# One more drain of GpSimd ahead of the last two reciprocal roots of a decoder layer

## The chip, the core and the metric

The kernel runs on one core of a Trainium2 chip. The metric is the device time of one execution in microseconds (us). Engines are named as in the profile: PE is TensorE (matrix products), DVE is VectorE, ACT is ScalarE, POOL is GpSimd, SP is SyncE, which here only issues transfers. A letter q behind an engine's name means its sequencer: the instructions that handle semaphores, drains and transfers and not data. Each engine works through its own queue in the order in which the program lists its instructions, and waits for the others through semaphores. A *drain* is an instruction that holds an engine's queue until the work issued before it on that engine is done.

## The reference

One layer of a decoder on 256 tokens of width 2048, in float32:

```
h = rmsnorm(x);  p = h @ w_in
A = dilated sliding-window attention (8 heads, three configurations merged)
B = latent attention (8 heads, low-rank q and kv, shared rotary key)
x = x + rmsnorm(concat(A, B) @ w_out)
u = square(relu(rmsnorm(x) @ w_up))          # 256 x 8192
x = x + rmsnorm(u @ w_down)                  # 256 x 2048, the output
```

rmsnorm(y) is y times 1/sqrt(mean(y*y) + 1e-6), row by row, times a gain. The change lies in the last line: the product with w_down and the norm behind it.

## The kernel before

Every float32 product is made of three products of halves: a value is split into hi (ACT rounds it, line 293) and lo (DVE takes the rest, line 294), and PE adds hi*hi, hi*lo and lo*hi (line 283). The weights come from memory as tiles called raw, on SP's queue. Some blocks of the two large products are done with seven products in place of eight ("seven" in the code); the sums that this needs take weights in pairs, which come through **GpSimd's queue** into tiles ab, ab_down, c and uT (line 360).

The product with w_down is made in two halves of 1024 output columns (c = 0, 1 in the code). In the first half the split of u is made by ACT and DVE and the lo part is kept in memory (ukeep); in the second half ACT makes hi again and GpSimd fetches lo back (line 935, tile ulo). In the same way line 390 fetches kept sums back (tile s). These three lines, 360, 935 and 390, hold all transfers that GpSimd issues. The last of them is the lo part of the last group of 512 rows (g = 15).

The last two groups of the second half (g = 14 and 15) come at the end, in the loop that the change touches. Its order is written out by hand: for each block b of 128 tokens and each half n of the columns it lists PE's products for four row blocks. In group 14 the seven-product part is then added by DVE (line 1214), and behind the first of these stands the fetch of group 15's lo part. In group 15 (products on line 1141) each finished quarter is squared and summed by ACT (line 1083) and multiplied with the gain by DVE (line 1087). When both quarters of a token block are done, `final(b)` makes the norm: DVE adds the sums up (lines 1092, 1093 and 1097, the last into t_fin), **GpSimd takes the reciprocal root** (line 1098, tile rstd_fin, one for each token block, hence two in all), DVE multiplies and adds the old x in five pieces (line 1104), and SP stores each piece (line 1106).

Behind `final`, the program closes: on the profile this is line 1248, where the layer's context ends. Each engine has a drain there and reports to a common semaphore; SP first waits for the landing of the last transfers; GpSimd waits for all engines, releases them, clears the semaphores, and the engines meet once more. No line of the kernel's own code is written for this.

On GpSimd's queue, from the last fetch on, there are: the fetch of ulo for group 15, the root for token block 0, the root for token block 1, and the closing.

Of the kernel before, what the change touches and what calls it, by code (L numbers as in the profile page):

```python
# [103 lines left out]
GT = FF // 512  # L104
# [146 lines left out]
def layer(nc, tc, io):  # L251
# [49 lines left out]
    def tok(t, k, b):  # L301
        return t[:, k, b * P:(b + 1) * P]
# [623 lines left out]
    def split_u(c, g):  # L926
        if (c, g) == (0, 0):
            uh, ul = [wp.tile([P, CW], F32R, tag=w, bufs=W_BUFS, name=f"u{w}0").rearrange("p (k s) -> p k s", k=4)
                      for w in ("hi", "lo")]
        else:  # L930
            uh, ul = [dpl["dp"].tile([P, 4, S], F32R, tag=f"u{w}", bufs=2, name=f"u{w}{c}_{g}") for w in ("hi", "lo")]
        u, h, l = [x.rearrange("p k s -> p (k s)") for x in (uT[g], uh, ul)]
        if c and g:
            nc.scalar.activation(h, u, AF.Copy)
            nc.gpsimd.dma_start(out=l.bitcast(F32), in_=ukeep[g])
        else:
            split(h, l, u)
        return uh, ul
# [134 lines left out]
    def down_mm(c, u, k, b, n, w, first, last):  # L1073
        three(y[b][2 * c + n], [tok(u[x], k % 4, b) for x in range(2)], [t[:, 0, n * 512:n * 512 + 512] for t in w],
              first, last)
# [5 lines left out]
    def square(n, b):  # L1081
        junk = dpl["dp"].tile([P, 512], BF16, tag="junk", bufs=1, name=f"junkd{n}{b}")
        nc.scalar.activation(junk, y[b][n], AF.Square, accum_out=ssd[b][:, n:n + 1])

    def gain(n, b):
        yg[n, b] = spare(2 * b, n)
        nc.vector.tensor_tensor(out=yg[n, b], in0=y[b][n], in1=spare(4, n), op=OP.mult)

    def final(b):

        part = con.tile([P, 2], F32, name=f"part{b}")
        nc.vector.reduce_sum(part[:, 0:1], ssd[b][:, 0:3], axis=mybir.AxisListType.X)
        nc.vector.tensor_scalar(part[:, 1:2], part[:, 0:1], 1.0 / D, EPS, op0=OP.mult, op1=OP.add)
        square(3, b)
        t = con.tile([P, 1], F32, tag="rs_f", bufs=2, name=f"t_fin{b}")
        r = con.tile([P, 1], F32, name=f"rstd_fin{b}")
        nc.vector.tensor_scalar(t, ssd[b][:, 3:4], 1.0 / D, part[:, 1:2], op0=OP.mult, op1=OP.add)
        nc.gpsimd.tensor_tensor(out=r, in0=t, in1=neg_half, op=OP.pow)
        gain(3, b)
        yield 0  # L1100
        for n, o, w in OUT_PIECES:
            c = slice(n * 512 + o, n * 512 + o + w)
            x = spare(6 + 2 * b, n)[:, o:o + w]
            nc.vector.scalar_tensor_tensor(out=x, in0=yg[n, b][:, o:o + w], scalar=r, in1=x,
                                           op0=OP.mult, op1=OP.add)
            nc.sync.dma_start(out=io["out"][b * P:(b + 1) * P, c], in_=x)
            yield 0
# [30 lines left out]
    def three_more(out, a, w):  # L1138

        for x, z in ((0, 0), (0, 1), (1, 0)):  # L1140
            nc.tensor.matmul(out, a[x], w[z], start=False, stop=(x, z) == (1, 0), skip_group_check=True)
            flow.spend(MM)
# [7 lines left out]
    for c in range(2):  # L1150
# [5 lines left out]
        for t, (what, k, tiles) in enumerate(wide_d[c]):  # L1156
            g = (2 * k if what == "w" else k) // 4
# [40 lines left out]

    tail = {k: tiles[0] for what, k, tiles in wide_d[1] if k >= 4 * (GT - 2) and what == "k"}
    for g in (GT - 2, GT - 1):  # L1200
        for b, n in PARTS:
            for kk in range(4):
                k = 4 * g + kk
                w = weights.get(tail[k])
                if g < GT - 1:
                    down_mm(1, us[1, g], k, b, n, w, False, kk == 3)
                else:
                    three_more(y[b][2 + n], [tok(us[1, g][x], kk, b) for x in range(2)],
                               [t[:, 0, n * 512:n * 512 + 512] for t in w])
                if (b, n) == PARTS[-1]:  # L1210
                    weights.free(tail[k])
                flow.pump()
            if g < GT - 1:
                nc.vector.tensor_tensor(out=y[b][2 + n], in0=y[b][2 + n], in1=more[b, n], op=OP.add)
                if (b, n) == (0, 0):
                    us[1, g + 1] = split_u(1, g + 1)
            elif n == 0:
                square(2, b)
                gain(2, b)
            else:  # L1220
                fin = flow.start(final(b))
# [22 lines left out]
def build(nc, arrays):  # L1244
    io = {n: nc.dram_tensor(f"in_{n}", a.shape, mybir.dt.from_np(a.dtype), kind="ExternalInput").ap()
          for n, a in arrays.items()}
    io["out"] = nc.dram_tensor("out_0", (S, D), F32, kind="ExternalOutput").ap()
    with tile.TileContext(nc) as tc, tc.manual_schedule():
        layer(nc, tc, io)
# [12 lines left out]
```

## Time and profile before

| what | value |
| --- | --- |
| device time, median of 3 runs | 1055.2 us (1055.2 to 1055.52) |
| span of the profiled execution, first to last instruction | 1053.8 us |
| mean granted clock of PE in it | 0.997 |
| busy: PE, DVE, ACT, POOL | 1040.8, 811.1, 625.1, 61.5 us |
| transfers issued by GpSimd | 98 |
| last fetch issued by GpSimd | at 1020.47 us |
| the two roots begin | at 1038.97 and 1044.40 us |
| last instruction of DVE ends | at 1047.8 us |

For the profiled execution the profile gives the span and no device time of its own; the runs' median is 1.4 us longer than that span. Times within the profile count from the span's start. A row of a timeline gives start, length, engine, line, operation, the tile written and the tiles read, and in brackets how long the engine had been idle and what ended that. Matrix products overlap, so PE's busy time is not PE at its peak. The page doesn't count semaphore, drain and transfer-issuing instructions as busy; they are found by asking for their line.

### The profile page before, as it was taken

To read this page: it belongs to the slowest core of one execution; us is meant where nothing else is said; L and a number is where in the kernel's file an instruction comes from. 1 tells how busy PE (TensorE), PEld (TensorE's weight loads), DVE (VectorE), ACT (ScalarE), POOL (GpSimd) and SP (SyncE) were. 2 spreads that over 40 slices of the span, in tenths; PEclk is the share of its full clock that TensorE was granted. 3 is DMA by queue.
4 is the path that set the end of the run, shared out by engine and by line. 5 is a ranking of instruction groups with operands and counts; after the bars stand their busy time and mean duration, and the time that the engine had idled before them with its cause. 6 is when DMAs were issued, how large, how long until landed. Compare 5 with 4: busy or idle time off the path is not lost.

```text
span 1053.8 us, 13458 instructions
## 1 busy us (share of the span) xinstructions
PE 1040.8 (99%) x4854; PEld 867.4 (82%) x4854; DVE 811.1 (77%) x1080; ACT 625.1 (59%) x834; POOL 61.5 (6%) x116
## 2 busy tenths in 40 slices
PE   9999999999999999999999999999999999999996
PEld 6888889888888788888888888888888888888884
DVE  6676536567557679879888798887899987989994
ACT  6584536565555467566665666566666664666671
POOL 0000000000000000000000100000000001212100
PEclk9999999999999999999999999999999999999998
DMA  9974447454447295647556466469779767789952
GB/s 296 361 233 146 143 130 241 143 162 159 140 171 231 78 347 167 224 142 239 185 198 200 154 222 217 139 223 318 256 274 317 263 216 271 254 297 327 375 167 80
DMA packets 80644, 229.34 MB, mean 218 GB/s; under 512 B 7617, under 2 KB 12225, under 8 KB 80193
## 3 DMA queue, kind: packets, MB, share of 16 engines
q1 hardware_dynamic: 65888, 176.45, 49.3%
q0 software_dynamic: 14112, 51.39, 14.2%
q8 instruction: 38, 0.62, 0.2%
q10 hardware_dynamic: 576, 0.64, 0.2%
q14 instruction: 30, 0.24, 0.1%
HBM read 212.72 MB, written 15.73 MB: 217 GB/s over the span
## 4 chain that ended last, share of the span: by engine, by line
PE 96%; DVE 1%; issue 1%; DMA 0%; ACT 0%; POOL 0%; DVEq 0%; POOLq 0%; ACTq 0%
PE y L283 26%; PE acc_u L283 25%; PE acc_o L283 8%; PE m L283 5%; PE md L283 5%; PE acc_qk L283 4%; PE acc_v L283 4%; PE acc_ckv L283 2%; PE acc_ukv L283 2%; PE acc_q L283 2%; PE acc_cq L283 2%; PE acc_k L283 2%; PE acc_uq L283 2%; PE rt L287 1%; PE sc_b L283 1%
## 5 line engine op out<-in xcount | busy, mean ns | idle before, releaser
L294 DVE TENSOR_TENSOR lo<-raw,hi 128x1024 fp32r<-128x1024 f32 (+3 forms) x213 | 241.8, 1152 | 92.5 <-ACT hi L293 91.9
L293 ACT ACTIVATE hi<-raw 128x1024 fp32r<-128x1024 f32 (+3 forms) x213 | 209.4, 999 | 78.3 <-PE y L283 20.8
L283 PE MATMUL acc_u<-hi,hT_hi 128*128 128x512 f32 x386 | 153.4, 397 | 0.0
L283 PE MATMUL acc_u<-hi,hT_lo 128*128 128x512 f32 x386 | 150.9, 391 | 0.4 <-DVE hT_lo L294 0.4
L283 PE MATMUL acc_u<-lo,hT_hi 128*128 128x512 f32 x386 | 150.5, 390 | 0.0
L283 PE MATMUL y<-hi,uhi 128*128 128x512 f32 x376 | 146.6, 390 | 0.0
L283 PE MATMUL y<-hi,ulo 128*128 128x512 f32 x376 | 146.3, 389 | 0.0
L283 PE MATMUL y<-lo,uhi 128*128 128x512 f32 x376 | 146.3, 389 | 0.0
L298 DVE SCALAR_TENSOR_TENSOR lo<-raw,gcol,hi 128x1024 fp32r<-128x1024 f32 x86 | 107.6, 1281 | 10.6 <-ACT hi L297 10.3
L297 ACT ACTIVATE hi<-raw,gcol 128x1024 fp32r<-128x1024 f32 x86 | 97.6, 1151 | 26.6 <-PE acc_u L283 13.2
L283 PEld LDWEIGHTS acc_u<-hi,hT_lo 128*128 128x128 f32 x386 | 72.5, 188 | 16.1 <-DVE hT_lo L294 0.8
L283 PEld LDWEIGHTS acc_u<-hi,hT_hi 128*128 128x128 f32 x386 | 72.6, 188 | 14.3 <-DVE c L1008 0.4
L283 PEld LDWEIGHTS acc_u<-lo,hT_hi 128*128 128x128 f32 x386 | 72.6, 188 | 14.2
L283 PEld LDWEIGHTS y<-hi,ulo 128*128 128x128 f32 x376 | 70.6, 188 | 14.6
L283 PEld LDWEIGHTS y<-hi,uhi 128*128 128x128 f32 x376 | 70.6, 188 | 14.6
L283 PEld LDWEIGHTS y<-lo,uhi 128*128 128x128 f32 x376 | 70.6, 188 | 14.5
L283 PE MATMUL acc_o<-hi,mixT_hi 128*128 128x512 f32 x128 | 51.8, 405 | 0.0
L294 DVE TENSOR_TENSOR lo<-st_down,hi 128x1024 fp32r<-128x1024 f32 x40 | 48.1, 1221 | 4.0 <-ACT hi L293 3.8
L283 PE MATMUL acc_o<-hi,mixT_lo 128*128 128x512 f32 x128 | 50.2, 392 | 0.0
L283 PE MATMUL acc_o<-lo,mixT_hi 128*128 128x512 f32 x128 | 50.0, 391 | 0.0
L293 ACT ACTIVATE hi<-st_down 128x1024 fp32r<-128x1024 f32 x40 | 42.1, 1052 | 11.1 <-PE y L283 9.5
L293 ACT ACTIVATE hi<-ab 128x512 fp32r<-128x512 f32 (+1 forms) x38 | 31.9, 842 | 28.2 <-PE acc_u L283 21.7
(322 smaller groups left out, 1989.3 us busy)
## 6 DMA issues: line engine op xcount, KB each, us to landing
raw<-in_w_down SPq DMA_DIRECT2D x88, 512.0 KB, 6.2
raw<-in_w_up SPq DMA_DIRECT2D x86, 512.0 KB, 4.5
raw<-in_w_in SPq DMA_DIRECT2D x55, 512.0 KB, 5.0
ab<-in_w_up POOLq DMA_DIRECT2D x36, 512.0 KB, 4.8
raw<-in_w_out SPq DMA_DIRECT2D x32, 512.0 KB, 4.4
ab_down<-in_w_down POOLq DMA_DIRECT2D x20, 512.0 KB, 6.7
ukeep<-ulo SPq DMA_DIRECT2D x15, 512.0 KB, 7.2
ulo<-ukeep POOLq DMA_DIRECT2D x15, 512.0 KB, 5.3
```

The lines of the kernel that those rows point to most:

```text
L283: nc.tensor.matmul(out, a, b, start=start, stop=stop)
L287: nc.tensor.transpose(out, a, ident)
L293: nc.scalar.activation(hi, src, AF.Copy)
L294: nc.vector.tensor_tensor(out=lo, in0=src, in1=hi.bitcast(F32), op=OP.subtract)
L297: nc.scalar.activation(hi, src, AF.Copy, scale=g)
L298: nc.vector.scalar_tensor_tensor(out=lo, in0=src, scalar=g, in1=hi.bitcast(F32), op0=OP.mult, op1=OP.subtract)
```

## The change

One instruction is added, `nc.gpsimd.drain()`. It is issued once, when the loop reaches the last group, g = GT - 1 = 15. At that point all of GpSimd's transfers have been listed and the two roots haven't. Nothing else differs.

```diff
     tail = {k: tiles[0] for what, k, tiles in wide_d[1] if k >= 4 * (GT - 2) and what == "k"}
     for g in (GT - 2, GT - 1):
+        if g == GT - 1:
+            nc.gpsimd.drain()
         for b, n in PARTS:
             for kk in range(4):
                 k = 4 * g + kk
```

## The prediction

> **What bounds the kernel now.** I began with the profile's page. The lines are the span, PE's busy time, the make-up of the chain that ended last, and (from the chain in order of time) its last pieces: start, length, what.
>
> ```profile
> span 1053.8 us, 13458 instructions
> ...
> PE 96%; DVE 1%; issue 1%; DMA 0%; ACT 0%; POOL 0%; DVEq 0%; POOLq 0%; ACTq 0%
> ```
> ```profile
> 1044.37 0.59 POOLq L1248
> ...
> 1046.39 1.45 DVE uT L1104 x3
> ```
>
> PE carries 96% of the chain, so up to the last product the kernel is bound by TensorE. But this chain stops at 1046.39 + 1.45 = 1047.84 us, and the span at 1053.8. The last 6 us hold no arithmetic, and a change on GpSimd has to be read there. Line 1248 is where the program closes (queues are emptied, the engines meet, semaphores are cleared). So next I asked for that line's instructions by short stretches; columns are engine, operation, count, then shortest, median and longest duration in ns, then first and last start. The first fence is the stretch 1044.9 to 1046, the second 1048 to 1051, the third 1051.05 to 1051.06, the fourth 1053.08 to 1053.09, the fifth 1053.1 to 1053.4.
>
> ```profile
> L1248 POOLq DRAIN  x1: 8672/8672/8672, 1044.4 to 1044.4; - x1
> L1248 DVEq DRAIN  x1: 2901/2901/2901, 1045.0 to 1045.0; - x1
> ```
> ```profile
> L1248 SPq EVENT_SEMAPHORE  x9: 28/28/28, 1048.5 to 1050.9; - x9
> ```
> ```profile
> L1248 SPq DRAIN  x1: 7/7/7, 1051.1 to 1051.1; - x1
> ```
> ```profile
> L1248 POOLq EVENT_SEMAPHORE  x1: 17/17/17, 1053.1 to 1053.1; - x1
> ```
> ```profile
> L1248 POOLq DRAIN  x1: 102/102/102, 1053.3 to 1053.3; - x1
> ```
>
> DVE's closing drain ends at 1045.0 + 2.9 = 1047.9, with DVE's last instruction. SP waits for the landing of the output, then reports with a 7 ns drain that lies at 1051.05 to 1051.06 (it appears in that stretch, not in the one before). GpSimd's closing drain begins at 1044.37 (the chain's row gives the hundredths), right behind its last reciprocal root, and ends at 1044.37 + 8.67 = **1053.04**. GpSimd's event semaphore, where the engines meet, comes at 1053.08. So GpSimd is the last to arrive, 2.0 us after SP. The waits of SP's queue say the same from the other side; its longest wait there is 2.2 us (the view names PE's queue as releaser, which had long been done):
>
> ```profile
> SPq L1248 <- PEq L1248: 2.7, 2, 2.2
> SPq L1248 <- DMA out<-uT: 1.9, 1, 1.9
> ```
>
> **What is in those 8.67 us?** The timeline of GpSimd: start, length, line, work, and in brackets the idle time before it.
>
> ```profile
> 1010.27 0.72 POOL L935 DMA_DIRECT2D ulo<-ukeep  x1 [9.66 <-PE y L283]
> 1020.47 0.54 POOL L935 DMA_DIRECT2D ulo<-ukeep  x1 [9.48 <-PE y L283]
> 1038.97 0.56 POOL L1098 TENSOR_TENSOR rstd_fin<-t_fin,neg_half 128x1 f32<-128x1 f32 x1 [17.96 <-DVE t_fin L1097]
> 1044.40 0.54 POOL L1098 TENSOR_TENSOR rstd_fin<-t_fin,neg_half 128x1 f32<-128x1 f32 x1 [4.87 <-DVE t_fin L1097]
> ```
>
> The second root ends at 1044.94, so 8.1 us of the drain follow it with no arithmetic on the engine. GpSimd has issued six groups of transfers by then, and its only other drains are the program's opening one (186 ns, before any transfer) and those behind the long one (102 ns above):
>
> ```profile
> L360 POOL DMA_DIRECT2D ab<-in_w_up x36 | 19.6, 544 | 250.6 <-DVE lo L294 222.9 <-DVE c L963 27.7
> L360 POOL DMA_DIRECT2D ab_down<-in_w_down x20 | 10.7, 538 | 111.5 <-PE acc_u L283 58.7 <-DVE lo L294 52.8
> L935 POOL DMA_DIRECT2D ulo<-ukeep x15 | 8.2, 550 | 111.0 <-PE y L283 91.9 <-DMA raw<-in_w_down 10.3 <-PE md L283 8.8
> L360 POOL DMA_DIRECT2D uT<-in_w_down x12 | 6.4, 538 | 0.0
> L360 POOL DMA_DIRECT2D c<-in_w_down x8 | 4.3, 538 | 64.1 <-DVE lo L294 55.8 <-DVE acc_u L909 8.3
> L390 POOL DMA_DIRECT2D s<-skeep x7 | 3.8, 538 | 52.8 <-PE md L283 52.8
> ```
> ```profile
> L1257 POOLq DRAIN  x1: 186/186/186, 0.3 to 0.3; - x1
> ```
>
> 36 + 20 + 15 + 12 + 8 + 7 = 98 transfers. The last was issued at 1020.47, and its landing time (below) is 6.2 us, so all had landed by 1026.7, 18 us before the drain. The drain therefore isn't waiting for data. My reading: it goes through the transfers issued since the last drain, 8.1 us / 98 = 83 ns each (an estimate from these rows); drains with none to go through take 0.1 to 0.2 us. That the drain behind the long one takes 102 ns says that what has been gone through once isn't gone through again.
>
> **The change, part by part.** One instruction is added, nothing is removed or moved. It stands on GpSimd's queue between the issue at 1020.47 and the root at 1038.97.
>
> *The early drain itself.* Its price isn't in the trace at this place. Lower bound: 0.2 us (no transfers). Upper bound: it first waits out the last transfer and only then goes through all 98. The landing, from the DMA view of 1019 to 1027 (KB, us to landing):
>
> ```profile
> ulo<-ukeep POOLq DMA_DIRECT2D x1, 512.0 KB, 6.2
> ```
>
> That is 1020.47 + 6.2 + 8.67 = 1035.3. I take the going-through as overlapped with the flight: 1020.5 + 8.7 = 1029.2. Either way GpSimd would have sat idle until 1038.97 (18 us, the root's row), so the cover is 3.6 to 9.8 us wide and the drain costs 0. Queued behind it are the two roots only; for them wait DVE's L1104 and then SP's stores. If the cover were gone, DVE has 0.83 us more before its next step is late:
>
> ```profile
> 1044.11 0.21 DVE L1097 TENSOR_SCALAR t_fin<-ssd,part 128x1 f32<-128x1 f32 x1 [0.83 <-ACT junkd L1083]
> ```
>
> So the drain would have to last beyond 1039.8, over 19 us, to delay the end.
>
> *The closing drain.* Ends of its price: 8.67 us (nothing taken over) and 0.6 us (the root's 0.54 us and 0.1 for an empty drain). I take the low end, as the 102 ns row is nearest: after the early drain only the root stands before it. It then ends near 1045.0, and GpSimd no longer arrives last. Little of this is needed: SP is last from the point where the closing drain ends before 1051.06, that is where 2.0 of its 8.1 us go (24 of 98 transfers at 83 ns).
>
> *What is late next.* SP, with the landing of the output: 1051.06. One hand-over to GpSimd follows; the nearest row is t_fin's end (1044.32) to the root's start (1044.40), 0.08 us, and 0.04 us lie between the long drain's end and the event semaphore. I take 0.05, with ends 0.02 and 0.1. The meeting comes at 1051.11 in place of 1053.08, and the 0.7 us behind it (1053.08 to 1053.8) follow unchanged. **Sum: -1.97 us**, span 1051.8.
>
> Does SP's arrival itself move? The long drain runs through the second half of the output's stores and not the first. DMA views, 1040 to 1043 (first half) and 1045 to 1048.45 (second):
>
> ```profile
> out<-uT SPq DMA_DIRECT2D x3, 256.0 KB, 2.6
> out<-uT SPq DMA_DIRECT2D x2, 128.0 KB, 2.7
> ```
> ```profile
> out<-uT SPq DMA_DIRECT2D x3, 256.0 KB, 2.5
> out<-uT SPq DMA_DIRECT2D x2, 128.0 KB, 2.7
> ```
>
> The same within 0.1, so the drain slows no stores, and taking it away speeds none. Single landings differ by 0.3 either way, which is the spread I give the sum.
>
> The span of the profiled execution is 1053.8 us; the runs' median, 1055.2, lies 1.4 above it, for what is outside the span. I leave that 1.4 alone: 1055.2 - 1.97 = **1053.2 us** (-0.19%).
>
> **The rivals.**
>
> *A. The 8.1 us have nothing to do with transfers that came before.* A drain of GpSimd behind arithmetic could have this price by itself, or could wait for the output's stores (the last SP wait is at 1050.9) plus 2 us. For: only one long drain exists, so a count of transfers as its cause isn't shown. Against: the drains of 0.1 and 0.19 us stand on the same engine, the first behind memsets. Then the early drain is hidden, the closing one still ends at 1053.04: 1055.2 us.
> The Trainium skill bears on this case: "PSUM — Partial Sum Buffer", Engine vs sequencer instructions, says that a "drain waits for the engine to go fully idle". By that alone the closing drain would end at 1044.94 and the early one at 1021.0; the long drain's row ends 8.1 us later, so either the trace doesn't agree or the engine wasn't idle in a way that the profile shows. Taken as it stands the rule gives no reason why an early drain should shorten the late one, which is this rival's 1055.2.
>
> *B. The early drain keeps DVE out (slower).* If going through the transfers blocks DVE's access to its operands, the block falls where the last weights are being split:
>
> ```profile
> 1017.79 3.49 DVE L294 TENSOR_TENSOR lo<-raw,hi 128x1024 fp32r<-128x1024 f32 x3
> 1021.65 1.23 DVE L294 TENSOR_TENSOR lo<-raw,hi 128x1024 fp32r<-128x1024 f32 x1 [0.37 <-ACT hi L293]
> 1022.79 2.28 DVE L1008 TENSOR_TENSOR uT<-md,uT 128x512 f32<-128x512 f32 x3
> 1025.10 0.69 DVE L1008 TENSOR_TENSOR uT<-uT,md 128x512 f32<-128x512 f32 x1
> 1025.70 2.35 DVE L294 TENSOR_TENSOR lo<-raw,hi 128x1024 fp32r<-128x1024 f32 x2
> 1027.97 1.29 DVE L1214 TENSOR_TENSOR y<-y,uT 128x512 f32<-128x512 f32 x2
> ```
> ```profile
> 1032.25 0.39 PE L1141 MATMUL y<-hi,uhi 128*128 128x512 f32 x1
> ```
>
> A block of 8.67 us from 1021.28 lasts to 1029.95; then 1.23 + 2.28 + 0.69 + 2.35 + 0.65 = 7.2 us remain to the first L1214, which ends at 1037.15 and not 1028.6. PE needs it at 1032.25 and stands 4.9 us; less the 1.97 at the end, +2.9: 1058.1 us. It decides from a block of 3.6 + 2.0 = 5.6 us on. Against it: DVE's L1104 runs before (1039 to 1043) and during (1044.9 to 1048) the long drain:
>
> ```profile
> L1104 DVE SCALAR_TENSOR_TENSOR uT<-c,rstd_fin,uT 128x512 f32<-128x512 f32 x2 | 1.4, 748 | 0.1
> ```
> ```profile
> L1104 DVE SCALAR_TENSOR_TENSOR uT<-c,rstd_fin,uT 128x512 f32<-128x512 f32 x2 | 1.4, 750 | 0.1
> ```
>
> 748 and 750 ns: no block. The Trainium skill ("SBUF — State Buffer", SBUF: two separate sides) has such a rule: GpSimd and a DVE instruction with two SBUF inputs take a shared port pair as "an exclusive lock, not a bandwidth split". L1104 has two such inputs, and the trace shows no lock by this drain.
>
> *C. The early drain lasts over 19 us* (its price grows beside the running transfers). At thrice 8.1 us it ends at 1044.8, both roots and the stores come 5 us later, SP arrives at 1056.1 and is last: 3.0 us slower, 1058.2. Nothing in the trace speaks for it.
>
> **How the numbers follow.** Forecast 0.76, A 0.17, B 0.05, C 0.02. The forecast's own range is 1052.6 to 1053.8 (the 0.3 of the landings, doubled, for one profiled execution against many timed ones). The range reaches up to A, since A alone holds 0.17: 1052.6 to 1055.4. A measurement of this kernel tells 0.2%, 2.1 us, from no change. The forecast's 1.97 lies just inside that: I give it 0.43 of being measured beyond (0.43 x 0.76 = 0.33). Faster 0.33; same 0.61 (the rest of the forecast, 0.43, with A, 0.17, and 0.01 of rounding); slower 0.06.
>
> **What the profile after would show.** Right: the three GpSimd drains on line 1248 and the new one, which is long (8 to 15 us) and begins near 1020.5; the first root still near 1039; the closing drain under 1 us; SP's 7 ns drain the last arrival, SP's longest wait behind it under 0.2 us. Wrong: a closing drain of 8 us again (A), DVE's rows between 1021 and 1030 longer or PE idle before 1032 (B), the first root late (C). A closing drain that is shorter by less than 2 us would mean that the 83 ns per transfer is no price per transfer.

## The result and the profile after

The kernel with the drain takes 1053.07 us (median of 19 runs, 1051.60 to 1053.61), the kernel before beside it 1054.85 us (19 runs, 1053.47 to 1055.65). The ratio is 0.9982 with a 95% interval of 0.9975 to 0.9989: 1.8 us faster. Both kernels vary by some 2 us from run to run, so the place of the gain has to be read inside one execution and not from two spans.

The page of the kernel after: the span, and the make-up of the chain.

```profile
span 1050.3 us, 13459 instructions
...
PE 96%; DVE 1%; DMA 1%; issue 1%; ACT 0%; POOL 0%; DVEq 0%; POOLq 0%; ACTq 0%
```

The timeline of GpSimd from the last fetch on (start, length, line, work):

```profile
1018.95 0.54 POOL L935 DMA_DIRECT2D ulo<-ukeep  x1 [9.48 <-PE y L283]
1037.45 0.56 POOL L1098 TENSOR_TENSOR rstd_fin<-t_fin,neg_half 128x1 f32<-128x1 f32 x1 [17.96 <-DVE t_fin L1097]
1042.88 0.54 POOL L1098 TENSOR_TENSOR rstd_fin<-t_fin,neg_half 128x1 f32<-128x1 f32 x1 [4.87 <-DVE t_fin L1097]
```

The span is 3.5 us shorter, more than the drain can account for. The last fetch, which comes ahead of the new drain, is at 1018.95 and was at 1020.47: 1.52 us earlier. The first root is earlier by the same 1.52 (1037.45 for 1038.97), and so is the second (1042.88 for 1044.40). So 1.52 us come from the stretch ahead of the drain, and most of them from the program's start: the first root that GpSimd takes at all (first fence before, second after) is already 1.14 us earlier, some 950 us ahead of the drain. That is the luck of these two executions. The remaining 2.0 lie behind the second root.

```profile
64.09 0.71 POOL L485 TENSOR_TENSOR rstd_pre<-t_pre,neg_half 128x2 f32<-128x2 f32 x1 [62.75 <-DVE t_pre L484]
```
```profile
62.95 0.71 POOL L485 TENSOR_TENSOR rstd_pre<-t_pre,neg_half 128x2 f32<-128x2 f32 x1 [61.61 <-DVE t_pre L484]
```

There the program now closes on line 1250. The first two fences are the added drain's line and the stretch 1042.80 to 1042.86; the next two are 1049.50 to 1049.52 and 1049.54 to 1049.55. Columns as before: count, shortest, median and longest duration in ns, first and last start.

```profile
L1202 POOLq DRAIN  x1: 9479/9479/9479, 1018.9 to 1018.9; - x1
```
```profile
L1250 POOLq DRAIN  x1: 644/644/644, 1042.8 to 1042.8; - x1
```
```profile
L1250 SPq DRAIN  x1: 7/7/7, 1049.5 to 1049.5; - x1
```
```profile
L1250 POOLq EVENT_SEMAPHORE  x1: 17/17/17, 1049.5 to 1049.5; - x1
```

The new drain takes 9.48 us at 1018.9, ends at 1028.4, and GpSimd idles until 1037.45. The closing drain falls from 8.67 to **0.64 us**, and the engines meet at 1049.54, 0.03 us after SP's report of 1049.51; before, it was 2.02 us (1051.06 to 1053.08). So 2.0 us are won in the closing. The waits of SP's queue in the closing show it from the other side: the two meetings cost it 2.7 us before and 0.7 now.

```profile
SPq L1250 <- DMA out<-uT: 1.9, 1, 1.9
SPq L1250 <- PEq L1250: 0.7, 2, 0.5
```

### The profile page after: what moved, and what is told of

Read it like the earlier page. It is cut to its first block, busy times and chain, and to the rows that moved or that the text cites. A ratio compares the mean times of both kernels' runs of the same rounds, so it can differ in the third digit from the quotient of the medians.

```text
span 1050.3 us, 13459 instructions
## 1 busy us (share of the span) xinstructions
PE 1039.0 (99%) x4854; PEld 865.9 (82%) x4854; DVE 811.0 (77%) x1080; ACT 625.4 (60%) x834; POOL 61.5 (6%) x116
## 4 chain that ended last, share of the span: by engine, by line
PE 96%; DVE 1%; DMA 1%; issue 1%; ACT 0%; POOL 0%; DVEq 0%; POOLq 0%; ACTq 0%
PE y L283 26%; PE acc_u L283 26%; PE acc_o L283 8%; PE m L283 5%; PE md L283 5%; PE acc_v L283 4%; PE acc_qk L283 4%; PE acc_ckv L283 2%; PE acc_ukv L283 2%; PE acc_q L283 2%; PE acc_cq L283 2%; PE acc_k L283 2%; PE acc_uq L283 2%; PE rt L287 1%; PE sc_b L283 1%
```

## The experiments

Two theories were set against each other. The first: a drain of GpSimd pays for each transfer that GpSimd has issued since its last drain, so the early drain takes this payment out of the closing into a stretch where GpSimd idles. The rival (A): the closing drain's price has nothing to do with the transfers before it. The diffs are against the kernel before, unless they show the change's own lines; each ratio is to the kernel before, run beside it.

### The drain in the middle

The change's drain is moved to the start of the second half of the product with w_down.

```diff
-        if g == GT - 1:
-            nc.gpsimd.drain()
...
     for c in range(2):
+        if c:
+            nc.gpsimd.drain()
         for i, (b, n) in enumerate(PARTS):
```

> The drain stands between the two halves of the product with w_down instead of at the end: 52 of GpSimd's 98 transfers lie before it, 46 behind. Price per transfer (83 ns each): the drain takes about 4.3 us at 834 us, where GpSimd idles for 44 us; the closing drain takes 0.6 + 46 x 0.083 = 4.4 us, ends near 1048.8, before SP at 1051.1, so the whole 2.0 us are won all the same: about 1.8 to 2.0 us faster than the kernel before. Theory A (the price does not depend on transfers before it): closing drain 8.7 us again, same time as before. A fixed price for any transfer at all since the last drain: closing drain 8.7 us again, same time.

1053.14 us, ratio to the kernel before 0.998 (0.9971 to 0.9989). The drain on the added line, the closing one, and SP's report:

```profile
L1152 POOLq DRAIN  x1: 10301/10301/10301, 819.9 to 819.9; - x1
```
```profile
L1249 POOLq DRAIN  x1: 4416/4416/4416, 1044.5 to 1044.5; - x1
```
```profile
L1249 SPq DRAIN  x1: 7/7/7, 1051.2 to 1051.2; - x1
```

The closing drain takes 4.42 us, as foretold for 46 transfers, and this is already enough for the whole gain: it ends at 1048.9, ahead of SP's report at 1051.2. What was missed is the early drain: it takes 10.3 us and not 4.3, and it stands at 819.9 and not at 834. It ends at 830.2, only 0.6 us before GpSimd issues its next fetch (830.80), so it was covered with little to spare. Its last transfer landed late; this is taken up under the last heading.

### A drain before any transfer

```diff
         rstd0.append(rstd_of(ss0, NB, D, "pre"))
+        nc.gpsimd.drain()
```

> The drain stands at 65 us, behind the first reciprocal root and before GpSimd has issued any transfer. Price per transfer: it takes under 0.3 us, and the closing drain 8.7 us as before: same time as the kernel before. If any earlier drain makes the closing one cheap (a first-call price of the instruction, paid once): it takes some 8 us here, the closing drain 0.6 us, and the kernel is 2.0 us faster.

1055.06 us, ratio 1.0000 (0.9991 to 1.0008).

```profile
L548 POOLq DRAIN  x1: 817/817/817, 63.2 to 63.2; - x1
```
```profile
L1249 POOLq DRAIN  x1: 8674/8674/8674, 1043.8 to 1043.8; - x1
```

The added drain takes 0.82 us, which holds the 0.71 us root in front of it (the drain's row begins as that root is handed out). The closing one takes 8.67 as before. So it isn't a price of the first drain, and a drain more doesn't help by itself.

### The drain behind the roots

```diff
     flow.finish(fin)
+    nc.gpsimd.drain()
     up.release()
```

> The drain stands behind both roots, directly ahead of the closing. Price per transfer: the added drain takes 8.7 us and the closing one about 0.1 us; GpSimd arrives as late as before, so the time is that of the kernel before plus 0.1 us at most: the gain comes from the place, not from the number of drains. Theory A in the form that a drain behind arithmetic has a price of its own: the added drain takes 8.7 us and the closing one again up to 8 us: up to 8 us slower.

1054.40 us, ratio 0.9997 (0.9988 to 1.0006). The added drain, the closing one, and SP's waits:

```profile
L1223 POOLq DRAIN  x1: 8672/8672/8672, 1042.0 to 1042.0; - x1
```
```profile
L1249 POOLq DRAIN  x1: 41/41/41, 1050.7 to 1050.7; - x1
```
```profile
SPq L1249 <- PEq L1249: 2.7, 2, 2.3
```

The same number of drains as in the change, and nothing won: the payment stands on the path whichever of the two makes it, and SP still waits 2.3 us. The run before this one shows that a drain behind arithmetic has no such price by itself, and this one that a drain more wins nothing by itself. What was left of rival A, a closing drain that waits for the output's stores and then for 2 us more, doesn't fit the two closing drains above that end ahead of SP's report (0.64 us in the change, 4.42 us with the drain in the middle). The price follows the transfers, and the gain follows the place.

### More transfers: 98 with a new tile

98 transfers of 16 numbers each are added to the kernel before.

```diff
         rstd0.append(rstd_of(ss0, NB, D, "pre"))
+        few = con.tile([P, 98], F32, name="few")
+        for i in range(98):
+            nc.gpsimd.dma_start(out=few[:16, i:i + 1], in_=io["consts"][:16, i:i + 1])
```

> No drain is added to the kernel before, but 98 more transfers of GpSimd, of 16 numbers each, issued between 65 and 120 us, where GpSimd idles; nothing reads them. Price per transfer whatever its size: the closing drain takes 0.6 + 196 x 0.083 = 16.8 us, ends near 1061.2, and the kernel is 8.1 us slower. Price by bytes or by rows of a transfer: closing drain 8.7 to 9.7 us, at most 1 us slower. Theory A: closing drain 8.7 us, same time.

1060.82 us, ratio 1.0058 (1.0044 to 1.0072): 5.8 us slower where the first theory said 8.1, and not for its reason. The closing drain:

```profile
L1251 POOLq DRAIN  x1: 6791/6791/6791, 1051.5 to 1051.5; - x1
```

It got shorter, 6.79 us and not 16.8, while it began 7.1 us later than in the kernel before (1044.4). Two things were mixed here, and the next two runs and the last one part them.

### 24 and 98 more without a new tile

The same transfers go into a tile that is there already and unused (24 in the one kernel, 98 in the other).

```diff
-    con.tile([P, 32], F32, name="con_pad")
+    pad = con.tile([P, 32], F32, name="con_pad")
...
+        for i in range(24):
+            c = i % 32
+            nc.gpsimd.dma_start(out=pad[:16, c:c + 1], in_=io["consts"][:16, c:c + 1])
```

> The kernel before with 24 more transfers of GpSimd, 16 numbers each, between 65 and 77 us, into columns of a tile that is there already and unused (so no tile moves to another address, as in the run with 98). Price per transfer whatever its size, 82 ns as the 98 and the 46 transfers gave it (8.03 and 3.77 us behind the root's end): the closing drain takes 0.6 + 122 x 0.082 = 10.6 us in place of 8.7, all of it behind SP: 1.9 to 2.0 us slower than the kernel before. Price by the rows or bytes that a transfer moves: closing drain 8.7 to 9.1 us, at most 0.4 us slower.

1056.56 us, ratio 1.0014 (1.0005 to 1.0023): 1.5 us slower for the 1.9 to 2.0 expected, which the interval covers (0.5 to 2.4 us). The closing drain, and SP's wait for the others:

```profile
L1251 POOLq DRAIN  x1: 10629/10629/10629, 1044.1 to 1044.1; - x1
```
```profile
SPq L1251 <- PEq L1251: 4.7, 2, 4.2
```

10.63 us, as foretold for 122 transfers; SP now waits 4.2 us. Each of the 24 moves 64 bytes in 16 rows where the kernel's own move 512 KB in 128, and the drain grew by (10.629 - 8.672) / 24 = 82 ns for each: the price is by transfer and not by bytes or rows.

> The same with 98 more, again without a new tile. The run with 98 more and a new tile had a closing drain of 6.8 us, worth 75 transfers at 82 ns, and lost 7 us along the whole kernel. If the count in that drain is bounded (transfers gone through before, without any drain, once there are too many): closing drain 6.8 us again, which is near SP's arrival, so 1.5 to 2.0 us faster than the kernel before, as far as the 7 us came from the moved tiles. If the 6.8 us came from the other layout: closing drain 16.8 us, 8 us slower. If the 7 us come from the transfers themselves: 5 to 7 us slower as in that run.

1053.56 us, ratio 0.9986 (0.9977 to 0.9995): *faster* than the kernel before, by 1.5 us, with 98 useless transfers more.

```profile
L1251 POOLq DRAIN  x1: 6792/6792/6792, 1043.2 to 1043.2; - x1
```

6.79 us again, the worth of 75 transfers out of 196. So the drain's count seems to be bounded: at some point between 122 and 196 transfers the older ones are dealt with without any drain. Where this happens, and what it costs there, I didn't follow.

### A quarter of the transfers before the drain

```diff
     evac = []
     for j in range(FF // CW):
+        if j == 5:
+            nc.gpsimd.drain()
         at = {bn: 4 * (j % 2) + i for i, bn in enumerate(PARTS)}
```

> The drain stands in the product with w_up, with 22 of the 98 transfers before it and 76 behind. Price per transfer: closing drain 0.6 + 0.07 + 76 x 0.082 = 6.9 us, which ends within 0.3 us of SP's arrival. A price in steps or a fixed one: 8.7 us.

A single execution, 1052.83 us. The early drain, the closing one, and SP's report:

```profile
L1018 POOLq DRAIN  x1: 6097/6097/6097, 560.4 to 560.4; - x1
```
```profile
L1250 POOLq DRAIN  x1: 6702/6702/6702, 1043.5 to 1043.5; - x1
L1250 SPq DRAIN  x1: 7/7/7, 1050.2 to 1050.2; - x1
```

In the trace 24 transfers were issued before the drain, two more than I had counted, which leaves 74. With the closing drain of the change (0 left, 0.644 us) as the base, the four kernels give (6.702 - 0.644) / 74 = 81.9, (4.416 - 0.644) / 46 = 82.0, (8.672 - 0.644) / 98 = 81.9 and (10.629 - 0.644) / 122 = 81.8 ns: **82 ns for each transfer**, a straight line.

### The cover taken away

The drain stands before the roots, but a copy of one column that DVE makes late holds it back.

```diff
+        if b == 0:
+            held = con.tile([P, 1], F32, name="held")
+            nc.gpsimd.tensor_copy(held, part[:, 1:2])
+            nc.gpsimd.drain()
         nc.gpsimd.tensor_tensor(out=r, in0=t, in1=neg_half, op=OP.pow)
```

> The drain stands ahead of the two roots as in the change, but is held until 1037 us by a copy of one column that DVE makes for the first norm: its cover is taken away. Price per transfer: it takes 8.1 to 8.4 us and ends near 1045.3, the first root comes 6.3 us late, DVE had 0.83 us to spare, so SP arrives 5.5 us later, near 1056.5, and the closing drain is under 1 us: 3.4 to 3.6 us slower than the kernel before. If the change gains by a drain anywhere before the closing, hidden or not: 2 us faster.

1067.14 us, ratio 1.0113 (1.0098 to 1.0129), more than three times the loss that was expected. The timeline of GpSimd:

```profile
1028.39 0.54 POOL L935 DMA_DIRECT2D ulo<-ukeep  x1 [9.48 <-PE y L283]
1044.82 0.18 POOL L1100 COPY held<-part 128x1 f32<-128x1 f32 x1 [15.89 <-DVE part L1093]
```

The last fetch, ahead of everything that was changed, is already at 1028.39 and not at 1020.47. The kernel is 7.9 us late before the drain begins, as the one with 98 transfers and a new tile was (its last fetch is at 1027.64, 7.2 us late). Both add a tile to the pool of constants. So I ran it again with the copied column in the tile that is there already (`pad[:, 0:1]` for `held`):

> The late drain once more, with the copied column in the tile that is there already, so that no tile moves. In the first late run the root came 6.3 us late and SP 5.5 us late counted from PE's last product, as foretold, but PE's products themselves ran 7.9 us late, before the drain had begun. Price per transfer with the cover gone: drain of 8.1 to 8.4 us, first root 6.3 us late, SP 5.5 us late, closing drain under 1 us; 3.4 to 3.6 us slower than the kernel before. If the drain itself were what slows PE: some 12 us slower again.

1058.16 us, ratio 1.0032 (1.0020 to 1.0045): 3.2 us slower. The drain, the timeline of GpSimd, DVE's wait, and the closing drain:

```profile
L1100 POOLq DRAIN  x1: 8299/8299/8299, 1035.0 to 1035.0; - x1
```
```profile
1035.04 0.18 POOL L1099 COPY con_pad<-part 128x1 f32<-128x1 f32 x1 [15.89 <-DVE part L1093]
1043.42 0.56 POOL L1101 TENSOR_TENSOR rstd_fin<-t_fin,neg_half 128x1 f32<-128x1 f32 x1 [8.20 <-issue]
```
```profile
DVE uT L1107 <- POOL rstd_fin L1101: 6.4, 1, 6.4
```
```profile
L1251 POOLq DRAIN  x1: 646/646/646, 1048.1 to 1048.1; - x1
```

The drain runs from 1035.0 to 1043.3, the root waits behind it, DVE stands 6.4 us. Of these 0.83 would have been DVE's spare time later, and 2.0 come back in the closing: 6.4 - 0.8 - 2.0 = 3.6 us expected, 3.2 measured. The same drain, with the closing one just as short, loses more than it wins once nothing covers it.

### One unused tile

```diff
+        if b == 0:
+            con.tile([P, 1], F32, name="held")
         nc.gpsimd.tensor_tensor(out=r, in0=t, in1=neg_half, op=OP.pow)
```

> The kernel before with nothing but one unused tile of one column in the pool of constants; no instruction is added. If the moved tiles are what cost 7 to 8 us in the two runs with a new tile: 7 to 8 us slower than the kernel before, spread over the whole kernel, with a closing drain of 8.7 us as before. If the added transfers or the late copy did it: same time.

1062.64 us, ratio 1.0076 (1.0062 to 1.0090): 7.7 us slower without one instruction more. From the timeline of GpSimd, an early root, a late one and the last:

```profile
209.70 0.69 POOL L485 TENSOR_TENSOR rstd_q<-t_q,neg_half 128x2 f32<-128x2 f32 x1 [24.56 <-DVE t_q L484]
...
382.35 0.54 POOL L485 TENSOR_TENSOR rstd_pre<-t_pre,neg_half 128x1 f32<-128x1 f32 x1 [10.03 <-DVE t_pre L484]
```
```profile
1046.23 0.56 POOL L1100 TENSOR_TENSOR rstd_fin<-t_fin,neg_half 128x1 f32<-128x1 f32 x1 [17.96 <-DVE t_fin L1097]
```

The last is 7.3 us later than in the kernel before (1038.97). It is the tile, then, that made the two kernels above 7 to 8 us late ahead of their last fetch, and not the transfers or the late copy.

## Why the prediction was right, point by point

**What the 8.67 us are.** Right, and now shown: a payment for transfers, made by the first drain behind them. The estimate was 83 ns a transfer, the slope of four kernels is 82.

**The closing drain.** Foretold 0.6 us, measured 0.64. That only 24 of the 98 had to go is borne out too: with 24 gone (the quarter, one execution) its closing drain ends at 1043.5 + 6.7 = 1050.2, with SP's report, and with 52 gone the gain is whole.

**What is late next.** SP, as foretold. The hand-over was taken as 0.05 us and is 0.03. I had written that SP's longest wait would be under 0.2 us; the view shows 0.5. That is the second meeting, which I had overlooked in this line; at the first one 0.2 of the 0.7 us are left.

**The early drain.** It cost nothing, as foretold, and lasted 9.48 us, within the ends of 0.2 and 14.8 (1020.5 to 1035.3) but longer than the 8.7 taken: the going-through isn't wholly hidden in the flight of the last transfer. With 9 us of idle time behind it this changed nothing.

**The sum.** Foretold -1.97 us and 1053.2; the closing lost 2.0 us in the profile, the medians differ by 1.8, and the median is 1053.07. That this lies so near 1053.2 is partly luck: the gain came out 0.2 us smaller, and the kernel before measured 1054.85 beside the change, 0.35 us under the 1055.2 that the sum started from. The 1.4 us between span and time, which the sum left alone, came from two different executions; within one execution of either kernel it is 1.7 to 1.85 us (1052.05 for the span of 1050.3 above). The interval, -0.25% to -0.11%, spans the 0.2% on whose near side the forecast lay.

**Rival A** said that the closing drain stays at 8.67 us, and it fell to 0.64 in the change itself; the drain before any transfer, the drain in the middle and the 24 transfers more rule out its other forms. The rule of the Trainium skill in "PSUM — Partial Sum Buffer", Engine vs sequencer instructions, holds for a GpSimd without transfers: the closing drain of the change ends within 0.1 us of the end of the root. With transfers it lacks the 82 ns for each, paid in the kernel before though the data had landed 18 us earlier.

**Rival B** fell in the change's own trace. DVE beside the early drain:

```profile
1020.20 1.23 DVE L294 TENSOR_TENSOR lo<-raw,hi 128x1024 fp32r<-128x1024 f32 x1 [0.45 <-ACT hi L293]
1021.34 2.28 DVE L1008 TENSOR_TENSOR uT<-md,uT 128x512 f32<-128x512 f32 x3
1023.66 0.69 DVE L1008 TENSOR_TENSOR uT<-uT,md 128x512 f32<-128x512 f32 x1
1024.26 2.35 DVE L294 TENSOR_TENSOR lo<-raw,hi 128x1024 fp32r<-128x1024 f32 x2
```

1.23, 2.28, 0.69 and 2.35 us, each as before. Line 294 has two operands in SBUF, and these rows show no sign of the lock that "SBUF — State Buffer" of the Trainium skill describes (SBUF: two separate sides). For a DVE instruction of this kind the page has the lock only against a GpSimd instruction that reads SBUF.

**Rival C** needed a drain of over 19 us and got 9.5. What C feared, a drain that holds up the roots, does cost time: the kernel with the cover taken away was 3.2 us slower. There the drain begins late, though, and lasts 8.3 us; no run has a drain of over 19 us.

A drain placed elsewhere should win no more here: with the closing drain out of the way SP's report sets the end, and that waits for the output's landing. The drain in the middle and the one of the change came out alike (0.9980 and 0.9982).

## What to carry to other kernels

Look behind the last arithmetic of a trace: the chain of waits stopped 6 us before the span's end, and the engine that arrived last there had nothing left to compute. If GpSimd has issued many transfers, its closing drain pays for them one by one; a drain in an earlier stretch where GpSimd idles for longer than that drain lasts (here 9.5 us for 98 transfers, 10.3 us for 52 whose last landed late) moves it off the path, and the same drain in front of work that others wait for costs more than it brings. When a kernel for comparison needs a small tile, take one that exists: a new one can move all others.

## What the runs showed of the hardware that was not expected

**Half of the payment comes behind the landing.** Three early drains, all begun while a transfer was still in flight, lasted longer than 82 ns a transfer. The last transfer ahead of each, its issue and its landing time (us), for the change, the drain in the middle and the quarter:

```profile
ulo<-ukeep POOLq DMA_DIRECT2D x1, 512.0 KB, 5.4
```
```profile
819.95 0.54 POOL L360 DMA_DIRECT2D c<-in_w_down  x1 [1.74 <-DVE lo L294]
```
```profile
c<-in_w_down POOLq DMA_DIRECT2D x1, 512.0 KB, 8.1
```
```profile
560.40 0.54 POOL L360 DMA_DIRECT2D ab<-in_w_up  x1 [0.59 <-DVE lo L294]
```
```profile
ab<-in_w_up POOLq DMA_DIRECT2D x1, 512.0 KB, 5.0
```

The landings are at 1024.4, 828.1 and 565.4; the drains end at 1028.4, 830.2 and 566.5, which is 4.1, 2.2 and 1.1 us later for 98, 52 and 24 transfers: 41, 42 and 45 ns each (the landing times are given to 0.1 us), half of the 82. It looks as if the transfers were gone through twice, once while the last is in flight and once more behind its landing. That fits all three; that there are two passes is an inference.

**The count seems to be bounded.** 196 transfers leave a closing drain of 6.79 us, in two kernels, shorter than that of 98. What bounds it is open. The executions of these two kernels take 2.0 to 2.1 us more than their spans, those of all others 1.7 to 1.85: some 0.3 us came back outside the span, for a reason that wasn't followed either.

**One column of an unused tile costs 7.7 us.** The lag grows along the whole kernel: against the kernel before, the root of the query latent (209.70 for 206.99) is 2.7 us late, the last root of the norms ahead of the product with w_up (382.35 for 377.76) 4.6, the last root 7.3. The time goes into PE's products: DVE and ACT are as busy as before (811.3 and 625.9 us for 811.1 and 625.1), PE is busy for 1047.6 us in place of 1040.8. One group of products, before (first fence) and with the tile (count, busy us, mean ns of one):

```profile
L283 PE MATMUL m<-hi,st 128*128 128x512 f32 x126 | 45.6, 389 | 0.0
```
```profile
L283 PE MATMUL m<-hi,st 128*128 128x512 f32 x126 | 46.5, 396 | 0.0
```

The added tile presumably moves the addresses of the tiles that come behind it. No run shows addresses, and why the products then take longer stays open.
